# A two-layer hybrid decoder trunk on one core: layer 0 reads x first and raw, the memory part comes later, values in groups of 512 columns

## The chip, the cores and the metric

The kernel runs on one core of one Trainium2 chip. The metric is the device time of one launch in microseconds. A core has five engines that run beside each other: TensorE (PE) multiplies matrices and transposes, VectorE (DVE) and ScalarE (ACT) work on elements, GpSimd (POOL) builds masks here, and SyncE (SP) issues transfers. Each engine takes the instructions of its own queue in order; semaphores let one wait for another.

## The reference

The input x has 512 tokens of width 1024 and goes through two layers. Each begins with a norm of x and one combined projection, and ends with a gated feed-forward part. In parallel with the token mixer, four heads attend to a memory of 256 rows:

```python
h = rms_norm(x, mix_norm_g[layer])
z = h @ hg_w_in          # layer 0: q | f | i | g | memory queries; layer 1: mla_w_in
y = hgrn2_mixer(z[..., :-256], ...)     # layer 0; layer 1: latent attention
m = memory_attention(z[..., -256:], rms_norm(mem, mem_norm_g[layer]), w_mem_kv[layer], ...)
x = x + concatenate([y, m]) @ w_out[layer]
x = x + conv_ffn(rms_norm(x, ffn_norm_g[layer]), w_up, conv_w, conv_b, w_down)
```

`rms_norm(x, g)` is x · rsqrt(mean(x²) + eps) · g. Its factor rsqrt(...) is one number for a token, so it may be applied to x or to the products of x with the weights. The recurrent mixer of layer 0 takes silu(q), a forget gate from f, values i and silu(g) as output gate, for six heads of 128 columns.

## The kernel before

**Products.** A float32 product is made of three float32r ones: both factors are split into a rounded part (hi) and a rest (lo), and hi·hi, hi·lo and lo·hi are added up in PSUM (`mm3`, L173 to L176 in the code). `gemm` (L242) does a group of columns of a weight matrix. A weight chunk of 512 KB comes by SP's queue into one of three `raw` buffers, ScalarE writes `whi` and VectorE `wlo` (two buffers of each), and TensorE multiplies: with tokens in the columns (512 wide), or, for values, memory queries and the keys of layer 1 (`tokens=True`), with weights in the columns, as wide as the group. PSUM has eight banks of 512 columns: four `acc` for products, two `at`, two `tp`; transposes go into `tp` and at the start `at` too. A split of x or of the memory (`split`, L193) reads a transposed tile from PSUM: ScalarE writes the hi part (xh, mth, cqh), VectorE the lo part (xl, mtl, cql), and then the bank is free.

**Order.** A scheduler puts the instructions of each engine into one row, which is then fixed; pools and buffers decide what may stand where. The program text gives it the order of the parts. `SCAN` (L82) is the order in layer 0: F, Q, V, G are the four groups of 256 columns (forget, query, value, gate) of a pair of heads 0, 1 or 2, L the seven levels of the recurrence, in which VectorE updates Kc, Qc and dn and TensorE makes small products, and N its end, with states (St), a norm by `ones` and the output y. `PRE` (L80) is the order at the start of layer 1: a and b project cq and ck, L loads the memory, u turns and splits it, p projects it, c and d turn cq and ck, n and m are norms, k makes keys, q queries.

**Start of layer 0.** SP loads parameters, the memory (two tiles of 512 KB), two chunks of its weights, then x in four tiles of 512 KB and the rest of the parameters. TensorE turns the memory (16 transposes) and projects it (48 products). Meanwhile x is squared, VectorE scales each tile of tokens by its norm (xn), and TensorE turns xn into the eight tiles xh/xl. After that come the memory queries as a group of 256 columns, 32 transposes of raw x, which VectorE copies into the residual X (L562, L563: two copies of 256 columns for each tile), the attention to the memory with the products of F0, Q0 and G0 beside it, and then the pairs by `SCAN`. Values are three groups (V0, V1, V2) of 96 products of 256 columns.

**Layer 1.** In `PRE` the memory is turned as a whole (u), then projected (p); the transposes of cq (c) come after that in the text, and the scheduler puts them between the products.

Of the kernel before, what the change touches and what calls it, by code (L numbers as in the profile page):

```python
# [16 lines left out]
P = 128  # L17
# [62 lines left out]
PRE = "a L b n u c p m d q k r"  # L80

SCAN = "F0 Q0 G0 L0 V0 F1 Q1 L1 N0 V1 G1 F2 Q2 N1 L2 V2 G2 N2"  # L82
# [14 lines left out]
def hybrid_trunk_kernel(ctx, tc, x, mem, params, pos, wts, out, tap):  # L97
# [208 lines left out]
    class Memory:  # L306
        def __init__(self, layer, pool):
            self.layer = layer
# [4 lines left out]
        def load(self, pool):  # L313
            self.mt = [pool.tile([P, D], F32, name=f"mt{b}") for b in range(2)]
            for b in range(2):
                nc.sync.dma_start(self.mt[b], mem[b * P:(b + 1) * P, :])

        def turn(self, pool):
            self.mth = [pool.tile([P, MEM], F32R, name=f"mth{d}") for d in range(KD)]
            self.mtl = [pool.tile([P, MEM], F32R, name=f"mtl{d}") for d in range(KD)]  # L320
            for d2 in range(KD // 2):
                ps = tp_tile()
                for d in range(2):
                    for b in range(2):
                        c = (2 * d2 + d) * P
                        transpose(ps[:, d * MEM + b * P:d * MEM + (b + 1) * P], self.mt[b][:, c:c + P])
                for d in range(2):
                    k = 2 * d2 + d
                    split(self.mth[k], self.mtl[k], ps[:, d * MEM:(d + 1) * MEM],
                          scale=pcol("memg", self.layer * KD + k, 1))  # L330

        def project(self):
            self.pk = [acc_tile(), acc_tile()]
            for c, kts in enumerate(PAIRS):
                hi, lo = chunk(f"w_mem_kv{self.layer}", 0, c)
                for j, kt in enumerate(kts):
                    for b in range(2):
                        r = slice(b * P, (b + 1) * P)
                        mm3(self.pk[b], self.mth[kt][:, r], self.mtl[kt][:, r], hi[:, j, :], lo[:, j, :],
                            kt == 0, kt == KD - 1)  # L340

        def keys(self, pool):
            layer, pk = self.layer, self.pk
            kv = pool.tile([P, 2, MW], F32, name="kv")
            kvf = pool.tile([P, D], F32, name="kvf")
            mss = sm.tile([P, 2], F32, name="mss")
            for b in range(2):
                act(kvf, self.mt[b], AF.Square, accum_out=mss[:, b:b + 1])
            rm = sm.tile([P, 2], F32, name="rm")
            rsqrt(rm, mss, D)  # L350
            for b in range(2):
                act(kv[:, b, :], pk[b][:, 0:MW], AF.Identity, scale=rm[:, b:b + 1])
                act(self.v[:, b, :], pk[b][:, MW:], AF.Identity, scale=rm[:, b:b + 1])
# [3 lines left out]
            kk = pool.tile([P, 2, MW], F32, name="kk")  # L357
            act(kk, kv[:, :, 0:MW], AF.Square)
# [15 lines left out]
        def queries(self, wname, group, xh, xl, tok, slot):  # L374
            self.qm = [slot(9 + i, F32) for i in range(2)]

            def evac(t, ps):
                dst = self.qm[t // 2][:, (t % 2) * MW:(t % 2 + 1) * MW]
                if tok is None:
                    act(dst, ps, AF.Copy)  # L380
                else:
                    act(dst, ps, AF.Identity, scale=tok[:, t:t + 1])

            gemm(wname, group, xh, xl, evac, tokens=True)
# [135 lines left out]
    with ExitStack() as l0:  # L520
# [4 lines left out]
        with tc.tile_pool(name="load", bufs=1) as lp, tc.tile_pool(name="mem0", bufs=1) as mp:  # L525
            memory = Memory(0, mp)
            with tc.tile_pool(name="mkt0", bufs=1) as mk:
                nc.sync.dma_start(par[:, :48], params[:, :48])
                memory.load(mk)
                for c in range(2):  # L530
                    chunk("w_mem_kv0", 0, c, ahead=True)
                xt = [lp.tile([P, D], F32, name=f"xt{t}") for t in range(NT)]
                for t in range(NT):
                    nc.sync.dma_start(xt[t], x[t * P:(t + 1) * P, :])
                nc.sync.dma_start(par[:, 48:], params[:, 48:])
                memory.turn(mk)
                memory.project()
                xn = []
                for t in range(NT):
                    xn.append(kq.tile([P, D], F32, name="xn", tag="Kc" if t < 2 else "Qc"))  # L540
                    junk = kq.tile([P, D], F32, name="junk", tag="Dg")
                    xss = sm.tile([P, 1], F32, name="xss")
                    act(junk, xt[t], AF.Square, accum_out=xss)
                    xr = sm.tile([P, 1], F32, name="xr")
# [512 lines left out]
```

## Time and profile before

| | |
|---|---|
| median of 3 runs | 1249.03 us (1248.24 to 1249.04) |
| the profiled execution | 1248.88 us |
| its span in the trace | 1246.8 us |
| TensorE busy | 1223.9 us (98%) |
| VectorE, ScalarE busy | 755.1 us, 558.5 us |
| data moved | 110.44 MB, mean 89 GB/s |

The profile is of one execution. Its span goes from the first to the last recorded instruction; the execution itself is 2.1 us longer. In a timeline each row gives the start, the duration, the engine, the line of the program, out<-in, and in brackets how long the engine was idle before and what it waited for. Matmuls overlap: the duration of one is longer than the distance to the next. The distance of two rows is therefore what a matmul costs in a run of them.

### The profile page before, as it was taken

The numbers are of one execution on the slowest core, as the hardware profiler recorded it, in microseconds if no ns is written. First come the engines' busy times: TensorE is split into PE (matmuls) and PEld (weight loads), VectorE is DVE, ScalarE is ACT, GpSimd is POOL, SyncE is SP. The second block draws the span as 40 slices with busy tenths as digits, with TensorE's granted clock in tenths as the row PEclk, the third lists the DMA queues.
The fourth block names the chain that finished last, engine by engine and source line by source line (L and its number), as shares of the span: only waits on it lengthen the run. The fifth ranks groups of instructions, "written<-read, shape, count | busy, mean of one in ns | idle before, by whom it ended". The sixth has DMA issues, their size and how long they took to land.

```text
span 1246.8 us, 15938 instructions
## 1 busy us (share of the span) xinstructions
PE 1223.9 (98%) x6106; PEld 1017.8 (82%) x6106; DVE 755.1 (61%) x1536; ACT 558.5 (45%) x966; POOL 18.7 (2%) x50
## 2 busy tenths in 40 slices
PE   6999999999999999999999999999999999999998
PEld 4869888888888888888889877777888888888887
DVE  6857575765776757652425758765665766764222
ACT  5463434433543434332325689754453444433211
POOL 6000000000000000000000000000000000000000
PEclk9999999999999999999999999999999999999999
DMA  6211222123232233323323312012223233322331
GB/s 238 80 52 60 77 68 69 53 84 91 96 101 101 85 102 101 97 90 101 102 85 111 119 33 77 33 34 68 85 85 102 87 102 99 102 94 92 116 120 51
DMA packets 31755, 110.44 MB, mean 89 GB/s; under 512 B 3776, under 2 KB 4160, under 8 KB 31680
## 3 DMA queue, kind: packets, MB, share of 16 engines
q1 hardware_dynamic: 31680, 109.43, 27.3%
q8 instruction: 48, 0.79, 0.3%
q14 instruction: 27, 0.22, 0.1%
HBM read 107.32 MB, written 2.10 MB: 88 GB/s over the span
## 4 chain that ended last, share of the span: by engine, by line
PE 92%; ACT 4%; DVE 3%; issue 1%; DMA 1%; SPq 0%; DVEq 0%; ACTq 0%
PE acc L171 63%; PE at L171 24%; PE tp L202 3%; PE tp L171 2%; ACT xl L191 1%; DVE wlo L179 1%; ACT whi L191 0%; ACT pr L191 0%; DMA mt<-in_mem 0%; ACT kv L191 0%; ACT yl L191 0%; ACT q L191 0%; ACT xh L191 0%; ACT yh L191 0%; PE at L202 0%
## 5 line engine op out<-in xcount | busy, mean ns | idle before, releaser
L179 DVE TENSOR_TENSOR wlo<-raw,whi 128x1024 fp32r<-128x1024 f32 (+2 forms) x201 | 240.0, 1195 | 374.5 <-ACT whi L191 367.3
L191 ACT ACTIVATE whi<-raw 128x1024 fp32r<-128x1024 f32 (+2 forms) x201 | 208.9, 1039 | 459.2 <-PE acc L171 298.8
L171 PE MATMUL acc<-xh,whi 128*128 128x512 f32 x616 | 241.1, 391 | 0.0
L171 PE MATMUL acc<-xh,wlo 128*128 128x512 f32 x616 | 240.8, 392 | 0.2 <-DVE wlo L179 0.2
L171 PE MATMUL acc<-xl,whi 128*128 128x512 f32 x616 | 240.9, 391 | 0.0
L171 PEld LDWEIGHTS acc<-xh,whi 128*128 128x128 f32 x616 | 115.7, 188 | 24.4 <-issue 1.0
L171 PEld LDWEIGHTS acc<-xh,wlo 128*128 128x128 f32 x616 | 115.5, 188 | 24.0 <-DVE wlo L179 0.4
L171 PEld LDWEIGHTS acc<-xl,whi 128*128 128x128 f32 x616 | 115.7, 188 | 23.6
L182 DVE SCALAR_TENSOR_TENSOR t<-u,par,t 128x510 f32<-128x510 f32 (+1 forms) x176 | 121.6, 746 | 4.2 <-ACT t L191 4.2
L171 PE MATMUL at<-xh,wlo 128*128 128x512 f32 x232 | 90.5, 390 | 0.0
L171 PE MATMUL at<-xl,whi 128*128 128x512 f32 x232 | 90.3, 389 | 0.0
L171 PE MATMUL at<-xh,whi 128*128 128x512 f32 x232 | 90.2, 389 | 0.0
L191 ACT ACTIVATE t<-u,par 128x512 f32<-128x512 f32 x88 | 67.0, 808 | 41.7 <-DVE u L179 41.7
L171 PE MATMUL acc<-wlo,xh 128*128 128x256 f32 (+2 forms) x224 | 67.1, 300 | 1.3 <-DVE wlo L179 1.3
L171 PE MATMUL acc<-whi,xh 128*128 128x256 f32 (+2 forms) x224 | 67.2, 302 | 0.5 <-ACT xh L191 0.4
L171 PE MATMUL acc<-whi,xl 128*128 128x256 f32 (+2 forms) x224 | 67.1, 301 | 0.0
L171 PE MATMUL acc<-whi,ah 128*128 128x512 f32 x132 | 51.3, 389 | 0.0
L171 PE MATMUL acc<-wlo,ah 128*128 128x512 f32 x132 | 51.3, 389 | 0.0
L171 PE MATMUL acc<-whi,al 128*128 128x512 f32 x132 | 51.3, 389 | 0.0
L171 PEld LDWEIGHTS at<-xl,whi 128*128 128x128 f32 x232 | 43.5, 188 | 9.1
L171 PEld LDWEIGHTS at<-xh,wlo 128*128 128x128 f32 x232 | 43.6, 188 | 9.0
L171 PEld LDWEIGHTS at<-xh,whi 128*128 128x128 f32 x232 | 43.5, 188 | 9.0
(333 smaller groups left out, 2143.4 us busy)
## 6 DMA issues: line engine op xcount, KB each, us to landing
raw<-in_w_up SPq DMA_DIRECT2D x88, 512.0 KB, 3.5
raw<-in_w_down SPq DMA_DIRECT2D x44, 512.0 KB, 3.5
raw<-in_hg_w_in SPq DMA_DIRECT2D x26, 512.0 KB, 3.6
raw<-in_w_out SPq DMA_DIRECT2D x16, 512.0 KB, 3.5
raw<-in_w_mem_kv SPq DMA_DIRECT2D x8, 512.0 KB, 4.6
mt<-in_mem SPq DMA_DIRECT2D x4, 512.0 KB, 4.7
xt<-in_x SPq DMA_DIRECT2D x4, 512.0 KB, 8.3
out<-u SPq DMA_DIRECT2D x8, 256.0 KB, 2.0
```

Of the source, the lines that this page charges most:

```text
L171: nc.tensor.matmul(ps, a, b, start=start, stop=stop)
L179: nc.vector.tensor_tensor(out=o, in0=a, in1=b, op=op)
L182: nc.vector.scalar_tensor_tensor(out=o, in0=a, scalar=s, in1=b, op0=op0, op1=op1)
L191: nc.scalar.activation(out=o, in_=a, func=f, **kw)
L202: nc.tensor.transpose(out=ps, in_=src, identity=ident)
```

## The change

**Layer 0 starts with x.** x comes in eight tiles of 128 x 512 (256 KB), four of its first half of width, a weight chunk, four of its second half, another chunk. The parameters are issued from ScalarE's queue. Raw x is turned and split with the gain (`mixg`) alone. The squares are summed for each token, one rsqrt gives `tok` (a factor for each token in a partition), and four transposes with a broadcast spread it into `bc`, the factor for each token in a column. Products with tokens in columns are multiplied by `bc` on VectorE (in `silu2` and `forget`, 18 times 512 columns); values and memory queries are scaled by `tok` on ScalarE when they leave PSUM.

**The memory part follows F0 and Q0.** `project` now also turns the memory, a pair of width tiles at a time, into two alternating buffers (mth0/mth1, mtl0/mtl1), and sums the squares after that. The part `u` of layer 1 is gone with it.

**Groups.** V0 and V1 are one group of 512 columns, V2 and the memory queries another, done before the attention. F1 stands beside the attention. Then come the 32 transposes of raw x for X, with half of the copies on ScalarE, and the rest by the new `SCAN`.

The diff, cut:

```diff
     w["hg_w_in"] = (("hg_w_in", 0), [
-        (_span(o + 256 * b, 256), QUADS) for b in range(3) for o in (768, 0, 1536, 2304)] + [(_span(3072, 256), QUADS)])
+        (_span(o + 256 * b, 256), QUADS) for b in range(3) for o in (768, 0, 2304)] + [
+        (_span(1536, 512), PAIRS), (_span(2048, 256) + _span(3072, 256), PAIRS)])
...
-PRE = "a L b n u c p m d q k r"
-
-SCAN = "F0 Q0 G0 L0 V0 F1 Q1 L1 N0 V1 G1 F2 Q2 N1 L2 V2 G2 N2"
+PRE = "a L b n c p m d q k r"
+
+SCAN = "G0 L0 V0 Q1 L1 N0 G1 F2 Q2 N1 L2 G2 N2"
...
-        def turn(self, pool):
-            self.mth = [pool.tile([P, MEM], F32R, name=f"mth{d}") for d in range(KD)]
-            self.mtl = [pool.tile([P, MEM], F32R, name=f"mtl{d}") for d in range(KD)]
-            for d2 in range(KD // 2):
+        def project(self):
+
+            pk = [acc_tile(), acc_tile()]
+            for c, kts in enumerate(PAIRS):
                 ps = tp_tile()
                 for d in range(2):
                     for b in range(2):
...
+                th = self.place(f"mth{c % 2}", [P, 2, MEM], F32R)
+                tl = self.place(f"mtl{c % 2}", [P, 2, MEM], F32R)
                 for d in range(2):
...
+                    split(th[:, d, :], tl[:, d, :], ps[:, d * MEM:(d + 1) * MEM],
+                          scale=pcol("memg", self.layer * KD + kts[d], 1))
                 hi, lo = chunk(f"w_mem_kv{self.layer}", 0, c)
...
+        xt = [[ld.tile([P, S], F32, name=f"xt{t}{i}") for i in range(2)] for t in range(NT)]
+        nc.scalar.dma_start(par[:, :48], params[:, :48])
+        for i in range(2):
+            for t in range(NT):
+                nc.sync.dma_start(xt[t][i], x[t * P:(t + 1) * P, i * S:(i + 1) * S])
+            chunk("hg_w_in", 0, i, ahead=True)
+        nc.scalar.dma_start(par[:, 48:], params[:, 48:])
+        xss = sm.tile([P, 2, NT], F32, name="xss", bufs=1)
+        for i in range(2):
+            ps4 = [at_tile(), at_tile(), tp_tile(), tp_tile()]
+            for t in range(NT):
+                for d in range(4):
+                    transpose(ps4[d][:, t * P:(t + 1) * P], xt[t][i][:, d * P:(d + 1) * P])
+            for d in range(4):
+                split(nh[4 * i + d], nl[4 * i + d], ps4[d], scale=pcol("mixg", 4 * i + d, 1))
+        for i in range(2):
+            for t in range(NT):
+                junk = kq.tile([P, S], F32, name="junk", tag="z")
+                act(junk, xt[t][i], AF.Square, accum_out=xss[:, i, t:t + 1])
+        tt(tok, xss[:, 0, :], xss[:, 1, :], ALU.add)
+        rsqrt(tok, tok, D)
+        spread(tok, 0, bc)
...
+        def silu2(ps, dst):
+
+            z = kq.tile([P, S], F32, name="z")
+            tt(dst, ps, bc, ALU.mult)
+            act(z, dst, AF.Tanh, scale=0.5)
+            stt(dst, z, 1.0, dst, ALU.add, ALU.mult)
...
+        got["F0"] = forget(0)
+        got["Q0"] = query(0)
...
+            memory.load()
+            memory.project()
+            memory.keys()
...
+            gemm("hg_w_in", 10, nh, nl, ev_v2, tokens=True)
+            memory.norms(slot)
+            memory.attend((0, 1), slot, yh, yl)
+            got["F1"] = forget(1)
+        for d in range(KD):
+            ps = tp_tile()
+            for t in range(NT):
+                transpose(ps[:, t * P:(t + 1) * P], xt[t][d // 4][:, d % 4 * P:(d % 4 + 1) * P])
+            act(X[:, d, :H], ps[:, :H], AF.Copy)
+            nc.vector.tensor_copy(out=X[:, d, H:], in_=ps[:, :H - 1:-1])
...
-                    "u": lambda: memory.turn(mk),
```

How the rows of three engines' queues stand before and after, at three places. A row gives the line of the program, the instruction and out<-in; x2 means twice in a row. The lines of the changed program are two higher.

First ScalarE's queue at the start. Before, from the first weight chunks on (xt are tiles of x, junk a square's unused output, xss its sum):

```order
L191 ACTIVATE whi<-raw 128x1024 x2
L191 ACTIVATE mth_205<-tp,par 128x256
L191 ACTIVATE mth_207<-tp,par 128x256
L191 ACTIVATE junk,xss<-xt_196 128x1024
L191 ACTIVATE mth_206<-tp,par 128x256
```

After, from the fifth row of work to the first splits of x (xt_182 to xt_188 are the second halves of x):

```order
L193 ACTIVATE le<-le 128x18
L193 ACTIVATE whi<-raw 128x1024
L193 ACTIVATE junk,xss<-xt_182 128x512
L193 ACTIVATE junk,xss<-xt_184 128x512
L193 ACTIVATE junk,xss<-xt_186 128x512
L193 ACTIVATE junk,xss<-xt_188 128x512
L193 ACTIVATE xh_149<-at,par 128x512
L193 ACTIVATE xh_150<-at,par 128x512
```

The first split that TensorE's products need, mth before and xh after, now has four squares of the second half of x right ahead of it.

Second ScalarE's queue in layer 1, from the last sum of squares of ck before the transposes. Before:

```order
L191 ACTIVATE junk,ssk<-ck 128x256
L191 ACTIVATE mth_5970<-tp,par 128x256
L191 ACTIVATE junk,ssr<-ck 128x64
L191 ACTIVATE mth_5972<-tp,par 128x256
L191 ACTIVATE junk,ssk<-ck 128x256
L191 ACTIVATE mth_5971<-tp,par 128x256
L191 ACTIVATE junk,ssr<-ck 128x64
L191 ACTIVATE mth_5973<-tp,par 128x256
L191 ACTIVATE whi<-raw 128x1024
```

After (the last row is the third pair of the memory):

```order
L193 ACTIVATE junk,ssk<-ck 128x256
L193 ACTIVATE cqh_5432<-tp,par 128x512
L193 ACTIVATE junk,ssr<-ck 128x64
L193 ACTIVATE cqh_5433<-tp,par 128x512
L193 ACTIVATE junk,ssk<-ck 128x256
L193 ACTIVATE whi<-raw 128x1024
L193 ACTIVATE junk,ssr<-ck 128x64
L193 ACTIVATE cqh_5434<-tp,par 128x512
L193 ACTIVATE mth_5787<-tp,par 128x256 x2
L193 ACTIVATE mth_5816<-tp,par 128x256 x2
L193 ACTIVATE whi<-raw 128x1024 x2
L193 ACTIVATE mth_5845<-tp,par 128x256
```

The three splits of cq moved ahead of the first of the memory, and a double whi stands ahead of the third pair's.

Third VectorE's queue at the end of the second pair's levels (L1). Before, from its last Qc row (tot is the total decay, wlo the lo part of the next weight chunk):

```order
L179 TENSOR_TENSOR Qc<-Qc,dn_1711 128x2x2x64
L179 TENSOR_TENSOR tot<-dn_1711 128x4
L179 TENSOR_TENSOR wlo<-raw,whi 128x1024
L182 SCALAR_TENSOR_TENSOR St<-St,tot,at 128x128
L179 TENSOR_TENSOR wlo<-raw,whi 128x1024
L182 SCALAR_TENSOR_TENSOR St<-St,tot,at 128x128 x3
L179 TENSOR_TENSOR oy<-tp,Gt 128x512
```

After:

```order
L181 TENSOR_TENSOR tot<-dn_1721 128x4
L181 TENSOR_TENSOR Gt<-acc,rbc 128x512
L184 SCALAR_TENSOR_TENSOR St<-St,tot,at 128x128
L181 TENSOR_TENSOR Gt<-acc,rbc 128x512
L184 SCALAR_TENSOR_TENSOR St<-St,tot,at 128x128
L184 SCALAR_TENSOR_TENSOR Gt<-z,Gt 128x512
L184 SCALAR_TENSOR_TENSOR St<-St,tot,at 128x128
L184 SCALAR_TENSOR_TENSOR Gt<-z,Gt 128x512
L184 SCALAR_TENSOR_TENSOR St<-St,tot,at 128x128
L181 TENSOR_TENSOR oy<-tp,Gt 128x512
L190 TENSOR_SCALAR rs_v<-tp 128x4
L181 TENSOR_TENSOR wlo<-raw,whi 128x1024
```

The rows of the output gate (Gt), all four St rows, oy and rs_v, the start of a norm on the sums by `ones`, moved ahead of wlo.

## Rows read from the trace of the kernel before

**Rows 1.** The page's first part: busy us, share of the span, instructions.
```profile
PE 1223.9 (98%) x6106; PEld 1017.8 (82%) x6106; DVE 755.1 (61%) x1536; ACT 558.5 (45%) x966; POOL 18.7 (2%) x50
```

**Rows 2.** Stretch, us, busy PE PEld DVE ACT POOL, PEclk, DMA share, GB/s.
```profile
10.59:16.74 6.15, 5.66 (x14) 3.75 (x15) 5.89 (x22) 3.22 (x7) 6.15 (x17) 1.00 1.03 412
...
31.04:296.40 265.36, 264.44 (x1596) 226.37 (x1597) 175.97 (x445) 117.50 (x214) 0.00 (x0) 1.00 0.23 70
...
655.00:849.00 194.00, 187.01 (x1087) 154.79 (x1087) 130.83 (x433) 137.60 (x365) 0.00 (x0) 1.00 0.21 65
```

**Rows 3.** Timeline of TensorE, start: start us, duration us, what, [idle before <-releaser].
```profile
10.59 0.79 PE L171 MATMUL acc<-whi,mth 128*128 128x512 f32 x1 [2.26 <-ACT mth L191]
...
16.52 0.58 PE L171 MATMUL acc<-whi,mtl 128*128 128x512 f32 x1
...
16.94 0.39 PE L171 MATMUL acc<-wlo,mth 128*128 128x512 f32 x1
...
17.17 0.40 PE L171 MATMUL acc<-whi,mtl 128*128 128x512 f32 x1
...
31.04 0.38 PE L171 MATMUL acc<-whi,xh 128*128 128x256 f32 x1 [0.43 <-ACT xh L191]
```

**Rows 4.** Timeline of TensorE, two unbroken runs of products, 256 and 512 columns.
```profile
35.03 0.28 PE L171 MATMUL acc<-whi,xh 128*128 128x256 f32 x1
...
38.86 0.28 PE L171 MATMUL acc<-whi,xl 128*128 128x256 f32 x1
...
237.15 0.39 PE L171 MATMUL acc<-xl,whi 128*128 128x512 f32 x1
...
245.54 0.39 PE L171 MATMUL acc<-xh,wlo 128*128 128x512 f32 x1
```

**Rows 5.** Timeline of ScalarE, start of the program.
```profile
5.06 1.06 ACT L191 ACTIVATE kvf<-mt 128x1024 f32<-128x1024 f32 x1 [2.98 <-DMA mt<-in_mem]
...
30.28 0.70 ACT L191 ACTIVATE xh<-at,par 128x512 fp32r<-128x512 f32 x1
...
33.87 0.62 ACT L191 ACTIVATE kk<-kv 128x512 f32<-128x512 f32 x1
```

**Rows 6.** Timeline of VectorE, split of x and copy into X.
```profile
31.02 0.75 DVE L182 SCALAR_TENSOR_TENSOR xl<-at,par,xh 128x512 fp32r<-128x512 f32 x1 [1.24 <-ACT xh L191]
...
46.56 0.41 DVE L562 COPY X<-tp 128x256 f32<-128x256 f32 x1
```

**Rows 7.** Timeline of TensorE in layer 1, first projections and memory projection.
```profile
662.91 0.44 PE L171 MATMUL acc<-wlo,xh 128*128 128x384 f32 x1 [1.34 <-DVE wlo L179]
...
689.50 1.04 PE L202 MATMUL tp<-ident,mt 128*128 128x128 f32 x8
...
691.27 0.50 PE L171 MATMUL acc<-whi,mth 128*128 128x512 f32 x1 [0.73 <-ACT mth L191]
...
704.88 1.03 PE L202 MATMUL tp<-ident,ck 128*128 128x128 f32 x8
```

**Rows 8.** Timeline of ScalarE in layer 1, at the memory projection.
```profile
690.75 0.47 ACT L191 ACTIVATE mth<-tp,par 128x256 fp32r<-128x256 f32 x1
...
693.05 1.07 ACT L191 ACTIVATE whi<-raw 128x1024 fp32r<-128x1024 f32 x1
...
698.00 1.36 ACT L191 ACTIVATE cqh<-tp,par 128x512 fp32r<-128x512 f32 x2 [0.96 <-PE tp L202]
```

**Rows 9.** Timelines of VectorE and TensorE, ends of L1 and L2 in layer 0.
```profile
163.51 1.22 DVE L179 TENSOR_TENSOR wlo<-raw,whi 128x1024 fp32r<-128x1024 f32 x1
...
164.67 0.35 DVE L182 SCALAR_TENSOR_TENSOR St<-St,tot,at 128x128 f32<-128x128 f32 x1
...
166.14 0.70 PE L171 MATMUL acc<-xh,wlo 128*128 128x512 f32 x2
...
168.19 0.69 DVE L179 TENSOR_TENSOR oy<-tp,Gt 128x512 f32<-128x512 f32 x1 [0.96 <-ACT osq L191]
...
234.00 2.35 DVE L179 TENSOR_TENSOR wlo<-raw,whi 128x1024 fp32r<-128x1024 f32 x2
```

More of the change, by code (lines that the diff above doesn't have):

```diff
@@ L524, in hybrid_trunk_kernel @@
         yl = {k: yp.tile([P, S], F32R, name=f"yl{k}") for k in (6, 7)}
[L525 to L544, printed above, removed]
-                    rsqrt(xr, xss, D)
-                    ts(xn[t], xt[t], xr, None, ALU.mult)
-                for d in range(KD):
-                    ps = tp_tile() if d % 2 else at_tile()
-                    for t in range(NT):
-                        transpose(ps[:, t * P:(t + 1) * P], xn[t][:, d * P:(d + 1) * P])
-                    split(nh[d], nl[d], ps, scale=pcol("mixg", d, 1))
-                memory.keys(mk)
-            with tc.tile_pool(name="mat", bufs=1, reuse_waits="tile") as mat:
-                def slot(i, dtype, n=1):
-                    return mat.tile([P, S] if n == 1 else [P, n, S], dtype, name=f"slot{i}")
-                memory.queries("hg_w_in", 12, nh, nl, None, slot)
-                for d in range(KD):
-                    ps = tp_tile()
-                    for t in range(NT):
-                        transpose(ps[:, t * P:(t + 1) * P], xt[t][:, d * P:(d + 1) * P])
-                    nc.vector.tensor_copy(out=X[:, d, :H], in_=ps[:, :H])
-                    nc.vector.tensor_copy(out=X[:, d, H:], in_=ps[:, :H - 1:-1])
-                memory.norms(slot)
-                memory.attend((0, 1), slot, yh, yl)
@@ new lines, in query @@
+        def query(b):
+            Qc = kq.tile([P, 2, S], F32, name="Qc")
+            gemm("hg_w_in", 3 * b + 1, nh, nl, lambda m, ps: silu2(ps, Qc[:, m, :]))
+            return Qc
+        got = {}
+        got["F0"] = forget(0)
+        got["Q0"] = query(0)
+        mp = lp.enter_context(tc.tile_pool(name="mem0", bufs=1))
+        with tc.tile_pool(name="mkt0", bufs=1, reuse_waits="tile") as mk:
+            memory = Memory(0, mp, lambda name, shape, dtype: mk.tile(shape, dtype, name=name, tag=name))
+            memory.load()
+            memory.project()
+            memory.keys()
@@ new lines, in hybrid_trunk_kernel, with slot, ev_v2 @@
+        with tc.tile_pool(name="mat", bufs=1, reuse_waits="tile") as mat:
+            def slot(i, dtype, n=1):
+                return mat.tile([P, S] if n == 1 else [P, n, S], dtype, name=f"slot{i}")
+            memory.query_tiles(slot)
+            def ev_v2(t, ps):
+                memory.put_queries(t, ps[:, 256:], tok)
+                act(v2[:, t, :], ps[:, :256], AF.Identity, scale=tok[:, t:t + 1])
+            gemm("hg_w_in", 10, nh, nl, ev_v2, tokens=True)
+            memory.norms(slot)
+            memory.attend((0, 1), slot, yh, yl)
+            got["F1"] = forget(1)
@@ L796, in hybrid_trunk_kernel @@
         mp = l1.enter_context(tc.tile_pool(name="mem1", bufs=1, reuse_waits="tile"))
-        memory = Memory(1, mp)
         def slot(i, dtype, n=1):
@@ L804, in hybrid_trunk_kernel @@
             with tc.tile_pool(name="mkt1", bufs=1, reuse_waits="tile") as mk:
+                memory = Memory(1, mp, lambda name, shape, dtype: mk.tile(shape, dtype, name=name, tag=name))
                 cq = zt.tile([P, NT, QLORA], F32, name="cq")
```

117 lines of the change are left out of this document (53 added, 64 removed).

## The prediction

> **What bounds the kernel now.** I read the engine totals first [rows 1]: TensorE is busy for 1223.9 of 1246.8 us, VectorE for 755, ScalarE for 559. TensorE sets the time, and only its gaps and its own matmul time can be changed. The table by stretches comes next [rows 2]: of the 22.9 us of gaps 0.9 lie between 31.04 us and the first up projection of layer 0 (264.44 of 265.36 busy), 7.0 in the mixer of layer 1, and the other 15.0 before 31.04 (where a cold clock loses more, below) and in the last stretch. So the change can win at the start, or by cheaper matmuls; in 31 to 296 us nothing is left to win but matmul time, and every new wait there is a loss. Then the timelines of single engines at the places where the change moves rows. All engines take their rows in order, so a row that waits holds back all behind it.
>
> **Start, term A: −2.2 us.** Before, TensorE's first product, on the memory, waits to 10.59 for its split, and the products then run cold: 16.52 to 16.94 is 0.42 us for one, the next to 17.17 takes 0.23 [rows 3]. (The granted clock reads 1.00 in this stretch too [rows 2]; the spacing shows the lower level.) At 31.04 it has done 48 products of 512 columns and 32 transposes, 48 × 0.227 + 32 × 0.11 = 14.4 us of work (eight transposes take 1.04, the last of them 0.27, so 0.11 a step [rows 7]); 16.6 us are lost. After, 48 products (F0) and 32 x transposes, with 4 small ones for the norm, are the first work. When can they start? The order of ScalarE after puts all eight squares, the four of the second half of x among them, ahead of the first split. SP queues 2.62 MB up to the last half tile (four halves, a weight chunk of 0.52 MB, four halves), and 0.42 MB of parameters come beside it. The first 0.55 MB was there at 5.06 [rows 5]; the other 2.5 MB at the 412 GB/s of the busiest stretch [rows 2] take 6.0: the last half is there at 11.1. A square of 512 takes 0.62, a split 0.70 [rows 5]; with hand-overs the first product starts at 12.65, against 10.59. If TensorE then stays cold as long as it did before (10.59 to about 16.8, 6.2 us), it does 3.1 us of work until 18.85; the rest of 48 × 0.227 + 20 × 0.11 = 13.1 us takes 10.0 more: 28.85 against 31.04. Bounds: −3.5 (half the cold stretch) to −0.5 (VectorE's xl, 0.75 each [rows 6], eight of them with two wlo of 1.2 in between, hold the products).
>
> **Columns, term B: −2.3 us.** Four groups of 96 matmuls of 256 columns become two of 96 of 512. From 35.03 to 38.86 lie 32 steps of 256 columns, 0.1197 us each; from 237.15 to 245.54 lie 37 of 512, 0.227 each [rows 4]. 384 × 0.1197 − 192 × 0.227 = 46.0 − 43.6 = 2.3. Both spacings are of a TensorE that waits for nothing, so this is gained if nothing new is waited for; bound 0.
> The Trainium skill, page "TensorE: Matmul & The Clock Gate", section "Back-to-back issue gap", gives a warm gap of N/2.4 ns plus 2.5, so 109.2 and 215.8 ns, by which two narrow ones cost only 2.5 ns more than a wide one: an estimate from that page is 0.5 us for the 192 pairs, and the sum below would be 1.8 higher. The rows show 10 ns and more beyond that formula for either width, and decide.
>
> **Norm on products: 0 by itself.** It removes four 1024-wide scalings, three of four rsqrt chains and adds 18 VectorE products of 512 columns, about 0.69 each like the product oy<-tp,Gt [rows 9]: 12.4 us on an engine that is busy 176 of 265 us in that stretch [rows 2]. Fourteen lie behind matmuls: 0 to +1, taken as 0. The four of G1 and G2 are costed at their place.
>
> **Memory in the middle of layer 0, term C: +1.9.** Before, it is part of the lost start. After, it stands between Q0 and the queries with nothing else on TensorE: 8 transposes, 24 products, 8 transposes, 24 products. On ScalarE the rows "whi of the second chunk" (its buffer comes free only when Q0's last product is done), and later "whi twice", stand ahead of the first split of each pair. Each time TensorE waits for a whi of 1.07 and a mth of 0.47 [rows 8], with hand-overs some 1.8, and its 8 transposes cover 0.8 to 0.9 [rows 7]: 0.9 and 1.0. Bounds 1.0 to 2.5.
>
> **X transposes, term F: +0.5.** All 32 now come in one burst with two banks. A tile takes TensorE four steps of 0.11, the copy of its half on VectorE 0.41 [rows 6] and on ScalarE 0.47 if it goes like the mth, also 256 columns from PSUM [rows 8], so a bank turns about as slowly again as it is filled, and the two copies run beside each other: 0 to 1.0.
>
> **Ends of the levels, terms P and H: +1.5 and +1.0.** Before, VectorE makes the next wlo at once after L1's last total, at 163.51, and one more with a single St row between; TensorE goes on with them at 166.14 [rows 9]. After, four Gt rows, four St, oy and rs_v stand ahead (0.69 for a Gt or oy row, 0.35 for an St one, some 0.07 less each in a queue: 4.2 us) and, since rs_v waits for the sums that TensorE itself makes, TensorE comes to F2's wlo with about 7.1 us of work for 9.8: it stands 2.7 where it stood about 1 at most: +1.5 (0.5 to 2.2). At the end of L2, before, TensorE has G2's products from 237.15 to 245.54 [rows 4] while VectorE makes two wlo in 2.35 [rows 9]; after, G2 is done by then, and eight products (1.8 us) stand before the first wlo of w_out, which VectorE has after Gt and St rows of 3.5 us: +1.0 (0 to 1.5).
>
> **Layer 1, term I: +4.0.** The diff only takes "u" from the list, yet it moves most. Before, 8 memory transposes follow the ck products at 689.50, and the first memory product starts at 691.27; the 12 cq transposes come later, between products [rows 7]. After, all 12 cq transposes come first with two banks, so the third tile waits for ScalarE's cqh and VectorE's cql of the first, and ScalarE has three cqh (1.36 for two), a whi of 1.07 [rows 8] and three sums of squares ahead of the first mth. By hand: cqh at 690.75 (where mth stood) and 691.56, a sum, whi to 693.5, a sum, the third cqh to 694.3, mth, first product 694.9. That is 3.6 later than 691.27; TensorE has then done 16 transposes instead of 8, 0.9 of that is not lost, and the cut into 4 + 8 hand-overs costs 0.3: +3.0. The double whi ahead of the third pair costs as in term C: +1.0. Nothing behind makes it up: from 691.27 to 704.88 TensorE does 13.1 us of work in 13.6 before [rows 7]. Bounds 1.5 to 5.
>
> **Sum.** −2.2 − 2.3 + 1.9 + 0.5 + 1.5 + 1.0 + 4.0 = +4.4. The profiled execution took 1248.88 us, 2.1 more than its span of 1246.8, and stands 0.15 below the median of 1249.03. So the span after is 1251.2 and the time, against the median, 1253.4 us.
>
> **Rivals.**
> One, *not slower*: the waits in layer 0 are covered. Place: memory part, X burst, ends of L1 and L2. If TensorE arrives there late by its own queue, with 2 us of products left when ScalarE and VectorE pass those rows, C, F, P and H (4.9) vanish: −0.5, so 1248.5. For it: before, TensorE lost only 0.9 us in all of 31 to 296 [rows 2], with similar chains. Against: those chains had queued products as cover, which the new order has used up.
> Two, *faster*: beside that, layer 1 costs 1.5 in place of 4.0, as its cq splits pass earlier: −3.0, so 1246.0.
> Three, *more slowly yet*: the clock. Before, TensorE works at 1.2 GHz after the idle start (the 0.42 us products [rows 3]) and at 2.4 from 16.94 on. If the gap of some 3 us in layer 1 has the same effect, its products double in length for up to 6 us: 3 us more, 1256.4. Against: TensorE still does transposes in that gap, and the largest gap of layer 1 before, 1.34 us at 662.91 [rows 7], left the stretch's mean clock at 1.00 [rows 2].
> The Trainium skill, same page, section "Why this matters for your kernels", wants no idle gaps between bursts of matmuls, as one puts the clock back to half; no row here shows it after the start.
> That the change doesn't do what it says: only the wide groups could fail, if the values wait for their wider evacuation; without B it is 1255.7, inside the forecast's range.
>
> **How the numbers follow.** Forecast (1251.5 to 1256, here 1253.4) 0.50, rival one 0.25, two 0.13, three with still longer waits 0.12. A measurement tells about 0.2% from no change, 2.5 us: faster is below 1246.5 (rival two, 0.13), same is up to 1251.5 (rival one, 0.25), slower is the rest, 0.62. The range reaches from 1246.5, which leaves most of rival two out, to 1258, rival three with some of the upper bounds.
>
> **What would show it.** First product on x at 12.65 (right: 12 to 13.5), F0 done by 29. TensorE's busy total less by some 2 us and its gaps beside the start more by 7 to 9. In layer 1 the last ck product to the first memory product: 5.4 us in place of 1.8. Gaps of about 1 us twice in each memory part, of 2 to 3 us ahead of F2, of 1 to 2 ahead of w_out. I am wrong if the first memory product of layer 1 follows within 3 us of ck's last, if F0 starts before 11, or if the clock falls again.

## The result and the profile after

The changed kernel takes 1262.47 us in the median of four runs (1259.83 to 1264.51) against 1249.03 of the kernel before: 1.0108 times as long, interval 1.0086 to 1.013. So it is slower, as forecast, but by 13.4 us and not by 4.4, and 4.5 us outside the range. The profiled execution (1264.51, span 1262.5) is the longest of the four; the readings below add up to its 15.7 us over the span before. The run of 1259.83 has a mean granted clock of 0.998 and the other three 0.994, so the clock is a part of what sets them apart; even that run lies 1.8 us above the range.

Page of the changed kernel, engine totals and clock over the span:

```profile
PE 1230.1 (97%) x5918; PEld 1012.3 (80%) x5918; DVE 759.8 (60%) x1509; ACT 566.2 (45%) x987; POOL 17.8 (1%) x50
...
PEclk9999899999999999999999999999999999999999
```

Against [rows 1], TensorE has 188 instructions less (192 fewer products, 4 more transposes) and yet is busy 6.2 us longer. That is the first hint: a product at the lower clock counts as busy for longer, so a fallen clock hides in the busy time. The fifth slice of the clock line shows one fall. The stretches of the changed kernel (columns as in [rows 2]) show three:

```profile
127.60:145.80 18.20, 16.07 (x94) 12.75 (x92) 17.36 (x54) 8.00 (x17) 0.00 (x0) 0.98 0.00 1
147.13:151.99 4.86, 4.86 (x12) 3.84 (x13) 2.15 (x5) 0.00 (x0) 0.00 (x0) 0.50 0.61 212
...
200.00:203.14 3.14, 3.14 (x10) 2.46 (x10) 1.14 (x7) 0.00 (x0) 0.00 (x0) 0.50 0.79 277
674.39:677.59 3.20, 3.20 (x11) 3.20 (x11) 3.10 (x23) 0.93 (x3) 0.00 (x0) 0.50 0.65 186
```

0.50 is 1.2 GHz. The products there stand 0.427 us apart (0.32 with 384 columns) in place of 0.227 (0.175): 2.0, 1.2 and 1.45 us lost, all of it "busy".

**Where the time went.** To put waits and clock into one measure, I took for each TensorE row the distance to the next start, less what that form takes in an unbroken run (0.227 for 512 columns, [rows 4]), and summed the excess by stretch, in us:

| stretch | before | after | difference | forecast |
|---|---|---|---|---|
| start to 30 us | 16.0 | 15.1 | −0.9 | A −2.2 |
| 30 us to the first level of L0 (memory, X) | 4.9 | 7.7 | +2.8 | C + F +2.4 |
| L0, to 14 us after its last total | 1.4 | 7.5 | +6.1 | none |
| L1, to 16 us after its last total | 2.0 | 5.5 | +3.5 | P +1.5 |
| rest of layer 0 to the norm | 2.6 | 3.8 | +1.2 | H +1.0 |
| start of layer 1 to the last ck product | 0.5 | 2.0 | +1.5 | none |
| last ck product to the transposes of ck | 1.4 | 5.3 | +3.9 | I +4.0 |
| rest | 21.1 | 20.8 | −0.3 | none |

That is +17.8. The work itself changes by −2.3 for the wide columns and +0.4 for the four transposes of the norm, so the sum is +15.9, against the 15.7 seen. The +1.5 at the start of layer 1 is the fall of the clock at 674.39. Landmarks that both kernels pass in the same order agree: the first product of the norm behind layer 0 comes at 312.4 instead of 301.4 (+11.0), ck's last product 12.4 later, the transposes of ck 16.3 later, and the lag then stays.

**The end of L0**, the largest item, on which the forecast had no term. TensorE, changed kernel:

```profile
144.02 0.71 PE L173 MATMUL at<-Qc,kp 128*128 128x128 f32 x4 [0.98 <-ACT kp L193]
147.13 0.80 PE L173 MATMUL acc<-wlo,xh 128*128 128x512 f32 x1 [2.39 <-DVE wlo L181]
147.72 0.63 PE L173 MATMUL acc<-whi,xl 128*128 128x512 f32 x1
148.15 0.63 PE L173 MATMUL acc<-wlo,xh 128*128 128x512 f32 x1
...
151.99 0.40 PE L173 MATMUL acc<-whi,xh 128*128 128x512 f32 x1
```

VectorE, changed kernel, at the same place (tot is the last row of the levels):

```profile
145.78 0.15 DVE L181 TENSOR_TENSOR tot<-dn 128x4 f32<-128x4 f32 x1
145.86 2.35 DVE L181 TENSOR_TENSOR wlo<-raw,whi 128x1024 fp32r<-128x1024 f32 x2
```

TensorE in the kernel before:

```profile
119.55 0.39 PE L171 MATMUL acc<-xl,whi 128*128 128x512 f32 x1
119.78 1.05 PE L171 MATMUL tp<-Ad,V 128*128 128x128 f32 x8
121.05 0.73 PE L171 MATMUL acc<-xh,wlo 128*128 128x512 f32 x2 [0.22 <-DVE wlo L179]
```

And the stretch of the levels in the kernel before:

```profile
101.30:119.70 18.40, 18.40 (x149) 17.76 (x148) 18.36 (x56) 7.73 (x18) 0.00 (x0) 1.00 0.09 29
```

The levels hold VectorE for 18.4 us before and 18.2 after, nearly full either way (18.36 and 17.36 us busy), and no wlo is made in them. TensorE's level products are some 6 us, so about 11 us of other products must cover the rest. Nearly all of them must come from weight chunks split beforehand, and there are two buffers: two chunks. (Of the chunk after these, a few products that need its whi alone can run ahead of its wlo.) Counted by form, before: 88 of V0's 96 products of 256 columns (10.5 us) and four of the next group stand inside the levels, 17.5 us of work in 18.4. After: the two chunks of the wide values are 48 products (10.9), but 16 of them are started before the levels begin, and the next chunk's wlo stands behind the levels. In the levels stand the other 32 and four of the next chunk on its whi alone (8.2 us), 14.4 us of work in 18.2. TensorE is out of work at 144.7, waits 2.39 us for a wlo, and works at 1.2 GHz behind the wait. The kernel before has one thing more at this place: V0 is complete by then, and eight products with it (119.78) stand in front of the wait while VectorE makes the wlo. After, half of the wide group is still to come, and nothing stands there.

### The profile page after: what moved, and what is told of

The parts are those of the page before. It is cut to its first block, busy times and chain, and to the rows that moved or that the text cites. A ratio compares the mean times of both kernels' runs of the same rounds, so it can differ in the third digit from the quotient of the medians.

```text
span 1262.5 us, 15563 instructions
## 1 busy us (share of the span) xinstructions
PE 1230.1 (97%) x5918; PEld 1012.3 (80%) x5918; DVE 759.8 (60%) x1509; ACT 566.2 (45%) x987; POOL 17.8 (1%) x50
## 4 chain that ended last, share of the span: by engine, by line
PE 92%; ACT 5%; DVE 2%; DMA 1%; issue 1%; SPq 0%; ACTq 0%; DVEq 0%
PE acc L173 63%; PE at L173 23%; PE tp L204 3%; PE tp L173 3%; ACT whi L193 1%; ACT xl L193 1%; DVE wlo L181 1%; DMA raw<-in_hg_w_in 0%; ACT junk L193 0%; ACT pr L193 0%; ACT yl L193 0%; PE at L204 0%; ACT q L193 0%; ACT kv L193 0%; ACT yh L193 0%
## 5 line engine op out<-in xcount | busy, mean ns | idle before, releaser
L173 PE MATMUL acc<-wlo,xh 128*128 128x512 f32 (+3 forms) x160 | 57.2, 357 | 3.7 <-DVE wlo L181 3.7
L173 PE MATMUL acc<-whi,xl 128*128 128x512 f32 (+3 forms) x160 | 57.6, 360 | 0.0
L173 PE MATMUL acc<-whi,xh 128*128 128x512 f32 (+3 forms) x160 | 55.1, 350 | 0.0
```

The costliest lines, as they stand in the source:

```text
L173: nc.tensor.matmul(ps, a, b, start=start, stop=stop)
```

## The experiments

They change the new kernel, except where the kernel before is named. "Lost" is the excess of the table above.

**l1_turn_first**: the memory of layer 1 is again turned as a whole ahead of the products.

```diff
-PRE = "a L b n c p m d q k r"
+PRE = "a L b n u c p m d q k r"
+        def turn_all(self):
+            self.turned = [self.turn(c, kts, 4) for c, kts in enumerate(PAIRS)]
```

> The changed kernel with one part of layer 1 undone: the memory is turned as a whole (u) ahead of its projection again; layer 0 as changed. Theory (the time is lost at single hand-overs that the order makes; in layer 1 from 689.5 to the ck transposes, 15.5 us before and 19.4 after): about 3.9 us faster than the changed kernel, some 1258.5, and the first memory product 1.8 us after the last ck product instead of 5.5. Rival (the loss in layer 1 is only moved from a later place, or is the clock's): under 1.5 us faster.

1259.41 us (1.0082, 1.0067 to 1.0097). TensorE in layer 1, changed kernel:

```profile
701.73 0.31 PE L173 MATMUL acc<-whi,xl 128*128 128x320 f32 x1
701.88 1.04 PE L204 MATMUL tp<-ident,cq 128*128 128x128 f32 x8
704.74 0.66 PE L204 MATMUL tp<-ident,cq 128*128 128x128 f32 x4 [1.82 <-DVE cql L184]
705.60 0.66 PE L204 MATMUL tp<-ident,mt 128*128 128x128 f32 x4 [0.20 <-DVE cql L184]
707.19 0.50 PE L173 MATMUL acc<-whi,mth 128*128 128x512 f32 x1 [0.94 <-ACT mth L193]
```

and with the memory turned first:

```profile
701.22 0.31 PE L173 MATMUL acc<-whi,xl 128*128 128x320 f32 x1
701.37 1.04 PE L204 MATMUL tp<-ident,mt 128*128 128x128 f32 x8
703.14 0.50 PE L173 MATMUL acc<-whi,mth 128*128 128x512 f32 x1 [0.73 <-ACT mth L193]
...
716.74 1.03 PE L204 MATMUL tp<-ident,ck 128*128 128x128 f32 x8
```

From ck's last product to the first one on the memory it is 1.92 us again instead of 5.46, as in [rows 7], and the loss up to ck's transposes is 1.4 again. The span is 4.4 shorter, the median 3.1. Term I is shown, in place and size.

**three_chunks**: three buffers each for whi and wlo in layer 0, two in a pool of their own behind it.

```diff
-        hi = wst.tile([P, 1024], F32R, name="whi", bufs=2)
-        lo = wst.tile([P, 1024], F32R, name="wlo", bufs=2)
+        hi = wsp[0].tile([P, 1024], F32R, name="whi")
+        lo = wsp[0].tile([P, 1024], F32R, name="wlo")
...
+        wsp[0] = l0.enter_context(tc.tile_pool(name='wsp3', bufs=3, reuse_waits='tile'))
...
+    wsp[0] = ctx.enter_context(tc.tile_pool(name='wsp2', bufs=2, reuse_waits='tile'))
```

> The changed kernel with three split weight chunks (whi, wlo) in layer 0 instead of two, from a pool of their own. Theory (during the levels VectorE makes no wlo, so TensorE lives on the chunks split before; two do not reach to the end of L0): the wait for wlo at the end of L0 (2.39 us at 147) and the cold stretch behind it (2.0 us) go, about 4 us faster, 1258.5. Rival (the levels themselves are what TensorE waits for, by kp): the wait only moves to the next kp product, under 1.5 us faster.

1254.63 us (1.0046, 1.0031 to 1.0061): 7.8 less than the changed kernel, the most of any single edit, and more than was expected. Its stretches:

```profile
126.30:143.90 17.60, 17.60 (x105) 14.85 (x104) 17.22 (x53) 8.21 (x17) 0.00 (x0) 1.00 0.00 1
143.90:160.00 16.10, 16.10 (x73) 13.33 (x72) 7.28 (x12) 5.84 (x7) 0.00 (x0) 1.00 0.41 131
```

VectorE is as full as before in the levels, but TensorE is busy throughout at full clock: L0 loses 0.7 instead of 7.5, L1 2.2 instead of 5.5. A part is given back at 296.04, where TensorE waits 2.23 us for a whi as the pool changes; after_three_turned, below, adds the third pair without that change of pools and has no such wait.

**x_copies_act**: all copies into X go to ScalarE, which leaves VectorE free for the levels earlier.

```diff
-            nc.vector.tensor_copy(out=X[:, d, H:], in_=ps[:, :H - 1:-1])
+            act(X[:, d, H:], ps[:, :H - 1:-1], AF.Copy)
```

> The changed kernel with all copies into X on ScalarE (after has half of them on VectorE). VectorE comes to the first level some 2.7 us earlier (8 rows of 0.34), and 10 more products of the values are left for the levels of L0 by the order. Theory (cover used up before the levels begin): the wait of 2.39 us at the end of L0 shrinks or goes, and with it the cold stretch; 2 to 5 us faster, 1257.5 to 1260.5. Rival (the copies on VectorE are hidden anyway and the wait is one for wlo whatever comes before): within 1 us of the changed kernel.

1262.04 us (1.0104, 1.0089 to 1.012), 0.4 less and inside the spread. The levels do start 2.1 us earlier (125.5 for 127.6) and L0 loses 5.6 for 7.5, but TensorE's wait behind them stays:

```profile
146.68 0.50 PE L173 MATMUL acc<-wlo,xh 128*128 128x512 f32 x1 [2.75 <-DVE wlo L181]
```

Only 4 of the values' products now stand ahead of the levels (16 in the changed kernel) and 48 in them (36), yet the levels last 19.9 us (18.2) and the wait for wlo is 2.75 (2.39). What L0 gains is the wait of 0.98 for kp and a shorter stretch at the lower clock. So how many of the products are used up ahead of the levels does not decide alone: the cover ends at two chunks wherever the levels stand.

**no_norm_products** leaves the norm out of the forget, query and gate columns (the 18 products with bc on VectorE).

```diff
-            tt(dst, ps, bc, ALU.mult)
-            act(z, dst, AF.Tanh, scale=0.5)
+            act(dst, ps, AF.Tanh, scale=0.5)
...
-                tt(z, ps, bc, ALU.mult)
```

> The changed kernel without the 18 VectorE products with the norm factor on forget, query and gate columns (the norm is left out of these columns); values and memory queries keep theirs. Theory (these products cost only where Gt rows stand ahead of what TensorE waits for: before the first level, at the ends of L1 and L2): 3 to 6 us faster, 1256.5 to 1259.5, in the ends of L0, L1 and L2. Rival (norm on products is the main cost: 12.4 us more of VectorE in a stretch it paces): 9 us faster or more, below 1253.5.

1258.61 us (1.0078, 1.0061 to 1.0095), 3.9 less. L1 loses 2.4 instead of 5.5; L0 keeps 5.3, with the same wait:

```profile
144.23 0.79 PE L173 MATMUL acc<-wlo,xh 128*128 128x512 f32 x1 [2.39 <-DVE wlo L181]
```

In this profile the clock fell at another place, behind the gap of layer 1: it is 0.50 from 697.24 to 704.07, the first memory products stand 0.427 us apart, and from ck's last product to the transposes of ck 7.6 us are lost in place of 5.3. So in that execution some 2.3 us of the gain are hidden.

"By itself 0" was wrong for the norm, but it isn't the main cause either. In L1 its rows are one condition of the loss and not the only one, since three_chunks (and values_256, next) bring L1 to 2.2 with the norm in place.

**values_256**: V0 and V1 are groups of 256 columns again.

```diff
-            (_span(1536, 512), PAIRS), (_span(2048, 256) + _span(3072, 256), PAIRS)])
+            (_span(1536, 256), QUADS), (_span(2048, 256) + _span(3072, 256), PAIRS), (_span(1792, 256), QUADS)])
-SCAN = "G0 L0 V0 Q1 L1 N0 G1 F2 Q2 N1 L2 G2 N2"
+SCAN = "G0 L0 V0 Q1 L1 N0 V1 G1 F2 Q2 N1 L2 G2 N2"
```

> The changed kernel with the values of pairs 0 and 1 as two groups of 256 columns again (chunks of four k-tiles, V1 after N0 as before); V2 and the memory queries stay one group of 512. Theory (TensorE lives through the levels on the two chunks split before them; V1 is work that stood behind L1): costs 96 x 2 x 0.1197 - 96 x 0.227 = 1.2 us of products, takes away most of L1's loss of 3.5 us and little at L0 (two chunks of 5.7 instead of 5.5 us): 1 to 3 us faster than the changed kernel, 1259.5 to 1261.5. Rival (the wide group itself is what leaves TensorE dry): 5 us faster or more, below 1257.5.

1259.54 us (1.0087, 1.007 to 1.0104), 2.9 less, with 1.2 us more of matmul time. L1 loses 2.2, as expected. But the theory expected little at L0, and most comes there: the wait is shorter and the clock stays up behind it, so L0 loses 3.0 instead of 7.5:

```profile
146.36 0.73 PE L173 MATMUL acc<-xh,wlo 128*128 128x512 f32 x2 [1.39 <-DVE wlo L181]
146.92 0.40 PE L173 MATMUL acc<-xh,whi 128*128 128x512 f32 x1
```

The median stays short of the rival's 5 us, but the width of the group is a part of the cause at L0.

**before_wide**: the kernel before with the wide groups alone (value and query groups as in the change).

> The kernel before with the wide groups alone (V0 and V1 one group of 512 columns, V2 with the memory queries another); x scaled and normed as before, the memory first, layer 1 as before. Theory: 2.3 us of products gained, of which the ends of L0 and L1 take some back, as two chunks split ahead last 10.9 instead of 11.5 us and V1 no longer stands behind L1: 1247.0 to 1249.5. Rival (the products' gain is whole): 1246.7. Rival (wide groups leave TensorE dry at the end of L0 as in the changed kernel, 6 us): 1252 or more.

1250.28 us (1.0008, 0.9999 to 1.0018, ten runs). The 2.3 us of term B are there as work, and are spent again: L0 loses 3.1 (1.4 before), L1 2.5, the rest of layer 0 3.6, and the clock falls to 0.50 from 663.8 to 667.0. At the end of L0 TensorE waits 1.69 us for a wlo (130.93) where it waited 0.22: the wide groups alone bring a part of what the changed kernel shows there, without the fall of the clock behind it.

**before_wide_three**: the same with a third pair of whi and wlo that takes every third chunk of layer 0.

```diff
+        third[1] += 1
+        pool, bufs = (third[0], 1) if third[0] and third[1] % 3 == 0 else (wst, 2)
-        hi = wst.tile([P, 1024], F32R, name="whi", bufs=2)
+        hi = pool.tile([P, 1024], F32R, name="whi", bufs=bufs)
```

> The kernel before with the wide groups and, in layer 0, a third pair of buffers for split weight chunks. Theory: nothing runs dry at the ends of the levels, the gain of the wide groups is whole and some of the 3 us that TensorE lost at the levels before goes as well: 1245.0 to 1247.0. Rival (three chunks only move the wait): as before_wide.

1249.29 us (1.0001, 0.9991 to 1.001), with runs from 1246.95 to 1250.54. L0 loses 1.1 and no wait for wlo is left at its end, but the time misses the expected 1245.0 to 1247.0. The difference to before_wide lies inside the spread; this pair of runs settles nothing alone.

**before_three**: the kernel before with the third pair alone.

> The kernel before with a third pair of buffers for split weight chunks in layer 0 and nothing else. Theory (before, little was lost at the ends of the levels, 6 us in all including small steps between products): 0 to 1.5 us faster than before, 1247.5 to 1249.0. Rival (the third pair alone explains the gain of after_three_turned): 1246.5.

1251.36 us (1.0022, 1.0012 to 1.0031), slower. L0 gains 0.6, but at 31.65 TensorE comes out of two waits, 1.11 for xn and 0.92 for xh, and works at 1.2 GHz for 3 us:

```profile
31.60:34.80 3.20, 3.15 (x15) 3.15 (x16) 3.20 (x5) 2.09 (x4) 0.00 (x0) 0.54 0.63 204
```

The clock is not all of it: two of the ten runs, with a mean clock of 0.999 and 1.0, still take 1250.45, 1.9 us more than the kernel before in the same series (median 1248.55). Why these waits grow with the third pair was not tried.

So more buffers are no gain by themselves. The kernel before had cover enough at L0; the change took it, and there the third pair pays.

**after_three_turned**: the changed kernel with the third pair in layer 0 and the memory turned as a whole in both layers, in layer 0 ahead of Q0.

```diff
         got["F0"] = forget(0)
-        got["Q0"] = query(0)
...
             memory.load()
+            memory.turn_all()
+            got["Q0"] = query(0)
             memory.project()
```

> The changed kernel with a third pair of buffers for split weight chunks in layer 0 (rotating with the two old ones, nothing new at the end of the layer), and with the memory turned as a whole ahead of its projection in both layers, in layer 0 ahead of Q0. Theory: against three_chunks (1254.6) the turn in layer 1 gives 3.9, the turn in layer 0 about 2, and the wait of 2.2 us where the pools changed goes: 1246.0 to 1248.0. Rival (these losses overlap with others): 1250 or more.

1246.49 us (0.9978, 0.9968 to 0.9987, ten runs): faster than both kernels. The lost time from 30 us to L0 goes from 7.7 to 5.2, in L0 to 0.9, in L1 to 2.1, and up to ck's transposes to 1.4; each is then within 0.5 of the kernel before, and the cheaper columns and the start are left as the gain.

**hold_clock**: 26 useless products of TensorE in the waits of L0's last levels, written to a bank that nothing reads.

```diff
+                        if b == 0 and h == 1 and lv > 4:
+                            idle = tp_tile()
+                            for _ in range(20 if lv == 6 else 6):
+                                mm(idle[:, :P], kp[:, :P], kp[:, P:], True, True)
```

> The changed kernel with 26 useless products of 128 columns (6 and 20) on the last two levels of L0, each group behind a product that TensorE has just done and in front of the one it waits for; the rows of all other engines stand as in the changed kernel. They fill the waits of 0.98 and 2.39 us and end before these do. Theory (the wait lets the clock fall, and the products from 147 to 152 at half rate cost 2.0 us of their own): about 2 us faster than the changed kernel, some 1260.5, granted clock 1.00 where it was 0.50. Rival (the clock falls for another reason, or the useless products only lengthen the wait): no change or slower.

1261.95 us (1.0105, 1.009 to 1.012). TensorE:

```profile
144.21 4.63 PE L173 MATMUL tp<-kp 128*128 128x128 f32 x40
148.60 0.48 PE L173 MATMUL acc<-wlo,xh 128*128 128x512 f32 x1
148.91 0.40 PE L173 MATMUL acc<-whi,xl 128*128 128x512 f32 x1
```

and the stretch behind the wait:

```profile
146.00:150.00 4.00, 4.00 (x32) 3.78 (x31) 2.96 (x6) 0.54 (x1) 0.00 (x0) 1.00 0.52 151
```

The fillers are twice as long as meant (two rows of 0.11 each) and overrun the wait: the first product comes at 148.60, not at 147.13, 1.47 late. But the clock stays at 1.00, and 2.0 us come back, −0.5 together: the products of the values end at 158.9 instead of 159.5. The median is 0.5 lower as well, but the two kernels' runs spread over 2.4 and 4.7 us, so that agreement is luck. All four profiles with this wait left open at 2.39 us or more (the changed kernel, l1_turn_first, x_copies_act, no_norm_products) have 0.50 behind it, and the one with fillers has not. So the fall goes with the idle time, and 2.0 us is its price in the changed kernel.

**best_hold**: after_three_turned with 11 such products in the 1.34 us wait at the start of layer 1.

> after_three_turned with 11 useless products of 128 columns in the 1.34 us wait of TensorE at the start of layer 1 (for wlo of the first projection). In the traces so far the same wait was followed by a stretch of 3.2 us at half clock in some (1.4 us) and not in others. Theory (the wait decides the clock by chance): the slower ones of its runs go, median 0 to 1 us below after_three_turned (1246.5), spread smaller. Rival: no change.

1246.39 us (0.9983, 0.9973 to 0.9992): no change, nor is the spread smaller. In the profile of after_three_turned the clock had not fallen at that wait, so there was nothing to hold.

**best_x_first**: after_three_turned with all of x ahead of the weight chunks in SP's queue.

```diff
                 nc.sync.dma_start(xt[t][i], x[t * P:(t + 1) * P, i * S:(i + 1) * S])
+        for i in range(2):
             chunk("hg_w_in", 0, i, ahead=True)
```

> after_three_turned with all eight half tiles of x loaded ahead of the first two weight chunks. Theory (the first product waits for the last squares, these for the last half of x): the last half lands 1.27 us earlier, first product at about 12 instead of 13.1, 0.5 to 1.2 us faster, 1245.3 to 1246.0. Rival (the weight chunk is then what comes last): no change.

1248.12 us (0.9997, 0.9987 to 1.0007), 1.6 more than without it. The chunk's split now comes last: VectorE makes wlo right ahead of the first xl, and TensorE waits 2.27 us (0.58 in after_three_turned); the first product comes at 13.15, not at about 12. VectorE:

```profile
14.72 1.21 DVE L181 TENSOR_TENSOR wlo<-raw,whi 128x1024 fp32r<-128x1024 f32 x1
15.85 1.40 DVE L184 SCALAR_TENSOR_TENSOR xl<-at,par,xh 128x512 fp32r<-128x512 f32 x2
```

## Why the prediction was right in sign and wrong in size

**The step that failed: "ends of the levels".** It looked at the ends of L1 and L2, where the order of VectorE's rows changes, and not at L0, where those rows stay as they were. It asked what stands ahead of the next wlo, not how much queued work TensorE has until then. That work is bounded by the two split chunks; before, it lasted through the levels (0.22 us of wait), after, it did not (2.39 us, and 2.0 at the lower clock). So +6.1 us had no term, and three_chunks takes it away. Why the chunks no longer last has more than one part. The width of the group is one: it brings 1.69 us of wait to the kernel before (before_wide), and without it the wait is 1.39 (values_256). The products used up ahead of the levels are another at most: with 4 of them in place of 16 the wait is still there (x_copies_act). How the 6.1 us divide between these was not tried. Rival one gave "those chains had queued products as cover, which the new order has used up" as its counterargument; that was the point, and it was not counted out.

**Rival three, the clock, holds at three other places.** "If the clock falls again" was the last of the forecast's own signs of being wrong, and it came. The rival put the fall behind the gap of layer 1 (where the clock stayed up, though it fell there in the profile of no_norm_products) and argued that the 1.34 us wait at 662.91 had done nothing. The same wait in the changed kernel,

```profile
673.86 0.45 PE L173 MATMUL acc<-wlo,xh 128*128 128x384 f32 x1 [1.34 <-DVE wlo L181]
```

is followed by 0.50 from 674.39 on. The three falls cost 4.65 of the 15.7 us of the profiled execution. The Trainium skill's rule against idle gaps (page "TensorE: Matmul & The Clock Gate", section "Why this matters for your kernels") that the forecast set aside for want of a row is borne out here in its direction: these three stretches, and hold_clock, are such rows. The waits in front of them, 0.64 to 2.39 us, are shorter than the gap that the section names, and there the measurement decides.

**A, the start: −0.9 instead of −2.2.** TensorE, changed kernel:

```profile
13.37 1.22 PE L173 MATMUL acc<-xh,whi 128*128 128x512 f32 x2 [4.33 <-ACT xh L193]
15.79 1.12 PE L204 MATMUL at<-ident,xt 128*128 128x128 f32 x4 [1.21 <-DVE xl L184]
```

VectorE there:

```profile
12.77 0.34 DVE L181 TENSOR_TENSOR xtok<-xss 128x4 f32<-128x4 f32 x1 [1.13 <-ACT junk L193]
...
14.82 0.26 DVE L184 SCALAR_TENSOR_TENSOR rs_t<-rs_t,rs_v 128x4 f32<-128x4 f32 x1
15.00 1.40 DVE L184 SCALAR_TENSOR_TENSOR xl<-at,par,xh 128x512 fp32r<-128x512 f32 x2
```

The squares ahead of xh were seen, and the first product came at 13.37 (forecast 12.65, bounds 12 to 13.5); F0's last product starts at 29.8, where F0 was to be done by 29. Not seen was that the rsqrt's tiny rows, 2.2 us in a chain, stand ahead of the first xl and hold TensorE for another 1.2.

**B** is right as work (−2.3), and "gained if nothing new is waited for" was the condition that failed; before_wide shows it spent even without the rest of the change.

**C and F**: +2.8 against 2.4. TensorE at the memory part of layer 0:

```profile
42.32 0.50 PE L173 MATMUL acc<-whi,mth 128*128 128x512 f32 x1 [0.41 <-ACT mth L193]
...
44.22 0.73 PE L173 MATMUL acc<-whi,mtl 128*128 128x512 f32 x2 [0.68 <-DVE mtl L184]
...
50.66 0.50 PE L173 MATMUL acc<-whi,mth 128*128 128x512 f32 x1 [0.69 <-ACT mth L193]
```

The waits are there, smaller and more of them than "about 1 us twice". No wait stands at the transposes of x (F): their excess is 0.5 us, 0.3 before.

**P**: +3.5 against 1.5, and by another way. Forecast was one wait of 2 to 3 us for F2's wlo. The trace has two short ones for ktok, and then the clock:

```profile
197.74 0.94 PE L173 MATMUL at<-v,ktok 128*128 128x128 f32 x6 [0.64 <-ACT ktok L193]
...
199.64 0.71 PE L173 MATMUL at<-v,ktok 128*128 128x128 f32 x2 [0.64 <-ACT ktok L193]
200.00 1.20 PE L173 MATMUL acc<-xh,wlo 128*128 128x512 f32 x2
```

No wait for F2's wlo is left, so the place was right and the row was not, and 1.2 of the term is the clock. ScalarE stood idle 1.37 and 1.41 us ahead of its ktok rows (197.19, 199.10), for transposes that TensorE itself makes: nothing was queued between these and the products with ktok, where the kernel before has four products (162.48 to 162.92). Without VectorE's norm rows, or with a third buffer, L1 loses 2.4 or 2.2; what empties the queue there was not tried further.

**H**: +1.2 against 1.0, but not by the wait that was forecast: TensorE comes to w_out's first products with wlo (260.27) without one, and the largest wait is 0.69 us for osq, ahead of the sums by `ones` (259.35). The size is luck.

**I**: +3.9 against 4.0, with 5.46 us from ck's last product to the memory's first (5.4 forecast). Of it 2.7 lie up to the first product on the memory and 1.2 behind (3.0 and 1.0 forecast); its working stands as it was.

**Busy total**: forecast 2 us less, measured 6.2 more, for the reason above. It is no test of work where the clock can move. The gaps beside the start grew by 9.7 us, from 12.0 to 21.7 (7 to 9 forecast). Nor does busy time show all that is lost without a fall: the forecast read 0.9 us lost from 31 to 296 before [rows 2], which is idle time alone; by the distances of the rows it is 10.9 up to the norm (the table above), mostly small steps.

## What to carry to other kernels

Where one engine's long stretch keeps it from preparing the next operands, count the work that the waiting engine has queued for that stretch: it ends at the number of prepared buffers, and another width of the groups, or another order elsewhere, can make it too short without touching a row there. Price a new wait of TensorE with what may follow it: here waits of 1.3 to 2.4 us (1.34, 2.39, and two of 0.64 close together) cost another 1.2 to 2.0 at the lower clock, hidden in the busy time. Wider products are a gain only while the queue behind them stays filled.

## What the runs showed of the hardware

The same wait does not always lower the clock. The 1.34 us wait at the start of layer 1 is (within 0.01) in all thirteen profiles without fillers there; the clock falls behind it in six (the changed kernel, l1_turn_first, x_copies_act, values_256, before_wide, hold_clock) and stays in seven others, the kernel before among them [rows 7]. The two waits of 0.64 us in L1 are the same in hold_clock as in the changed kernel, but in hold_clock no fall is behind them and L1 loses 4.0 instead of 5.5. There is one profile of each kernel, but the mean clock of every run is known. Of 25 runs of the kernel before (the series of hold_clock), three with a mean clock of 0.998 took 1250.29 to 1250.38 us and 22 with 0.999 or more 1247.92 to 1249.08. The step of at least 1.2 us is about the price of one such fall (1.45), so the execution decides at least in part; where in the program the clock fell in those three is not recorded.

Nor does the record of the clock always show what the spacing shows. The same stretch at the start, changed kernel:

```profile
16.00:20.00 4.00, 4.00 (x21) 3.44 (x21) 3.88 (x7) 2.83 (x4) 2.40 (x10) 1.00 0.46 186
```

and after_three_turned:

```profile
16.00:20.00 4.00, 4.00 (x18) 3.34 (x16) 3.72 (x7) 3.01 (x4) 3.38 (x10) 0.51 0.29 107
```

The first reads 1.00, though its product at 17.14 has the next row 0.42 us behind it, as the one at 16.24 in the second has (0.43). At the start of a program the spacing is the better witness.
